# A depthwise convolution of width 31 moved from vector instructions to 32x32 matmul tiles, inside a one-layer hybrid backbone

## The chip, the core and the metric

The kernel runs on one core of a Trainium2 chip. The core has five engines that take their instructions in order and wait for each other through semaphores: TensorE (PE in the profile; its weight loads are listed as PEld), VectorE (DVE), ScalarE (ACT), GpSimd (POOL) and SyncE (SP, which here only issues DMAs). The metric is the time of one execution on the device in microseconds; the smaller, the better. Matmul results land in PSUM, which this kernel cuts into eight banks of 128x512 fp32; everything else lives in SBUF or in HBM.

## What is computed

The layer has 512 latent tokens of width 1024 and 256 context tokens. One projection `w_in` feeds a state-space branch (S5), a convolution branch and two gates; the branches are merged, and a mixture of 32 experts follows. The change touches the convolution branch alone:

```python
def conv_branch(zb, n_rows, w_dw, b_dw, ln_g, ln_b, w_out):
    v = glu(zb)
    n_b, n_l, ch = v.shape
    v = v.reshape(n_b * n_rows, n_l // n_rows, ch)
    v = lax.conv_general_dilated(v, w_dw.astype(v.dtype)[:, None, :], window_strides=(1,), padding='SAME',
                                 dimension_numbers=('NWC', 'WIO', 'NWC'), feature_group_count=ch) + b_dw
    v = jax.nn.silu(layernorm(v, ln_g, ln_b))
    return v.reshape(n_b, n_l, ch) @ w_out
```

Here `ch` is 512, there are 8 rows of 64 tokens, and the filter has 31 taps. Every channel has its own filter, so a channel of the output is a sum of 31 shifted copies of the same channel of the input, each times one number.

## The kernel before

Activations lie with channels on the 128 partitions and the 512 tokens along the row, so the 512 channels of the convolution are four blocks `j` = 0 to 3 of 128x512.

The stretch that matters comes after the projection of the S5 input and before the merge. Its loop is written as a list of one-letter steps, `RaAaODPBbUVTCkaI`, run for `b` = 0 to 7. On PE and ACT the instructions stand in the order in which these steps are written (a manual schedule); on DVE, POOL and SP a scheduler orders them when the program is built, by priority and readiness, and the engines then run that fixed order. The steps that the prediction speaks of:

- A, B and C are tiles of the `w_in` projection, `z_tile(t)` (lines 754 to 774): 24 matmuls of 128x128 by 128x512 into one PSUM bank (`zp`), from weights split into a high part `zuwh` (ACT, line 751) and a low part `zuwl` (DVE, for eight of the tiles POOL, line 752) two tiles ahead. Tiles 0 to 7 are the convolution's GLU: an even one is kept, an odd one is passed through a sigmoid and multiplied with the even one before it into the padded buffer `vp` (line 770). Tiles 8 to 23 are gates. Tiles 0, 1 and 2 run ahead of the loop.
- I is `s5_in(b+2)` (lines 658 to 694): 16 matmuls (`pv`, line 666), then some sixteen DVE instructions with two scans (line 681) among them and a few on POOL, which give `st`. R is `s5_read(b)` (line 699 on, `py`), which uses what I made two rounds earlier. k is `s5_pk(b+2)` (line 546), b the transposes of `s5_pv` (line 533), V and P prepare S5 tables on POOL and DVE, O transposes S5 results (line 720).
- a is one step of a product that is worked off on the side, `ada` (lines 806 to 846): either four 128x32 matmuls `pma` (line 818) that DVE adds up in `adacc`, or scalings on ACT and additions on POOL.

The convolution of block j is written as closures: `conv_taps(j)` (lines 783 to 789) appends one `tensor_scalar` (tap 0 and the bias) and 30 `scalar_tensor_tensor` to the list `taps`, each of which multiplies a shifted 128x512 view of `vp` with a column of taps and adds to `cacc`. `tap(200)` after the loop writes them all out at the end of the block, and the scheduler then places all 124 among the other DVE instructions, where it sees room. After the loop `cacc` goes through a layernorm (line 995 on: `pmu`, `pvr`) while the S5 branch runs through its GLU (`pglu`).

SBUF tiles of 128x512 come from one pool tag, `s2`, with seven buffers; PSUM has four banks of tag `mm` (`zp`, `py`), two of `s5` and two of `tp` (transposes, `pk`, `pma`, `padr`).

Of the kernel before, what the change touches and what calls it, by code (L numbers as in the profile page):

```python
# [9 lines left out]
F32 = mybir.dt.float32  # L10
# [3 lines left out]
AF = mybir.ActivationFunctionType  # L14
ALU = mybir.AluOpType
# [11 lines left out]
def hybrid_kernel(  # L27
# [9 lines left out]
    V, S, G, T, SY = nc.vector, nc.scalar, nc.gpsimd, nc.tensor, nc.sync  # L37
    D = 1024
    L, LC = 512, 256
# [7 lines left out]
    TAPS, HALF = 31, 15  # L47
    ROWS, RW = 8, 64
# [12 lines left out]
    hstack = ExitStack()  # L61
    hp = hstack.enter_context(tc.tile_pool(name="hp", bufs=1))
    smstack = ExitStack()
    sm = smstack.enter_context(tc.tile_pool(name="sm", bufs=7, side="right"))
    ps = ctx.enter_context(tc.tile_pool(name="ps", bufs=4, space=PSUM))

    def t2k(name, dt=F32, cols=512, p=128):
        return sm.tile([p, cols], dt, tag="s2", name=name)

    def t4k(name):  # L70
        return sm.tile([128, 1024], F32, tag="ub", name=name, bufs=2)

    def ps_mm(name, p=128):
        return ps.tile([p, 512], F32, tag="mm", name=name, bufs=4)
# [4 lines left out]
    def ps_tp(name, p=128):  # L79
        return ps.tile([p, 512], F32, tag="tp", name=name, bufs=2)  # L80
# [114 lines left out]
    sel32 = sm.tile([128, 32], F32, tag="sel32", name="sel32", bufs=1)  # L195
# [4 lines left out]
    cwt = const.tile([128, 4, 32], F32, name="cwt")  # L200
# [7 lines left out]
    def col(nm, j):  # L208
        return cols[:, ROW[nm] + j:ROW[nm] + j + 1]
# [185 lines left out]
    def mm3(acc, wh, wl, ah, al, start, stop):  # L395
        T.matmul(acc, lhsT=wh, rhs=ah, start=start, stop=False)  # L396
        T.matmul(acc, lhsT=wh, rhs=al, start=False, stop=False)  # L397
        T.matmul(acc, lhsT=wl, rhs=ah, start=False, stop=stop)  # L398
# [318 lines left out]
    def s5_out(j):  # L717
        pt = ps_tp("pt")
        for t in range(TC):
            T.transpose(pt[:, 64 * t:64 * t + 64], ysb[j][:, t, :], ident[0:64, 0:64])  # L720
        y = sm.tile([128, L], F32, tag="yt", name="yt", bufs=1)
        S.activation(y.rearrange("p (c t) -> p c t", t=TC), pt.rearrange("p (t c) -> p c t", t=TC), AF.Copy)
        S.activation(yh[:, j, :], y, AF.Copy)
        V.tensor_tensor(yl[:, j, :], y, yh.bitcast(F32)[:, j, :], op=ALU.subtract)
# [17 lines left out]
    def z_load(t):  # L742
        if t < len(zt) and zt[t][0] not in zraw:
            zraw[zt[t][0]] = wload(f"zr{t}", w_in[0], zt[t][0])

    def z_split(t):
        if t < len(zt):
            c0, i, _ = zt[t]
            raw = zraw[c0][:, :, 128 * i:128 * i + 128]
            zu[t] = wpair(0, list(raw.shape[1:]), "zu")  # L750
            S.activation(zu[t][0], raw, AF.Copy)
            (G if t in ZPOOL else V).tensor_tensor(zu[t][1], raw, zu[t][0].bitcast(F32), op=ALU.subtract)  # L752

    def z_tile(t):
        z_split(t + 2)
        z_load(t + 4)
        w = zu.pop(t)
        c0, i, kind = zt[t]
        acc = ps_mm("zp")
        for k in range(KD):  # L760
            mm3(acc, w[0][:, k, :], w[1][:, k, :], hh[:, k, :], hl[:, k, :], k == 0, k == KD - 1)
        if kind == "a":
            zp.append(acc)
            return

        sg = t2k("sg")
        S.activation(sg, acc, AF.Sigmoid)  # L767
        if kind == "b":
            jb = t // 4
            V.scalar_tensor_tensor(vp[jb][:, i, :, HALF:HALF + RW], sg.rearrange("p (r t) -> p r t", r=ROWS), 0.0,  # L770
                                   zp.pop().rearrange("p (r t) -> p r t", r=ROWS), op0=ALU.add, op1=ALU.mult)
            conv_taps(2 * jb + i)
        else:
            SY.dma_start(out=gd[2 * kind + i], in_=sg)

    gd = dram.tile([16, 128, L], F32, name="gd")
    cacc = {}
    taps = []

    for j in range(2):  # L780
        cacc[j] = t4k("cacc").rearrange("p (a n) -> p a n", a=2)

    def conv_taps(j):
        src = vp[j // 2][:, j % 2]
        dst = cacc[j // 2][:, j % 2, :].rearrange("p (r t) -> p r t", r=ROWS)
        e = V
        taps.append(lambda: e.tensor_scalar(dst, src[:, :, 0:RW], cwt[:, j, 0:1], col("conv_b", j), op0=ALU.mult, op1=ALU.add))
        for k in range(1, TAPS):
            taps.append(lambda k=k: e.scalar_tensor_tensor(dst, src[:, :, k:k + RW], cwt[:, j, k:k + 1], dst, op0=ALU.mult, op1=ALU.add))  # L789

    def tap(n):
        for _ in range(min(n, len(taps))):
            taps.pop(0)()

    adr = dram.tile([8, 512], F32, name="adr")

# [75 lines left out]
    with tc.manual_schedule(engines=MANM):  # L872
        def zt_(t):
            if t < 24:
                z_tile(t)

        def in_(b):
            if b < NB:
                inp[b] = s5_in(b)

        def if_(f, b):
            if b < NB:
                f(b)

        MID = {"R": lambda b: s5_read(b, *inp.pop(b)), "U": lambda b: s5_ut(b + 2), "P": lambda b: if_(s5_pa, b + 2), "a": lambda b: ada(1),
               "A": lambda b: zt_(3 * b + 3), "B": lambda b: zt_(3 * b + 4), "C": lambda b: zt_(3 * b + 5),
               "O": lambda b: s5_out(b // 2) if b % 2 else None, "D": lambda b: if_(s5_bd, b + 2), "b": lambda b: if_(s5_pv, b + 2),
               "k": lambda b: if_(s5_pk, b + 2), "V": lambda b: if_(s5_vb, b + 3), "T": lambda b: if_(s5_pt, b + 2), "I": lambda b: in_(b + 2)}
        M0 = {"s0": lambda: z_split(0), "s1": lambda: z_split(1), "z0": lambda: z_tile(0), "z1": lambda: z_tile(1), "z2": lambda: z_tile(2),
              "i0": lambda: in_(0), "i1": lambda: in_(1), "bd1": lambda: s5_bd(1), "pt1": lambda: s5_pt(1), "pv1": lambda: s5_pv(1),  # L890
              "pk1": lambda: s5_pk(1), "vb2": lambda: s5_vb(2), "pv0": lambda: s5_pv(0), "pk0": lambda: s5_pk(0), "pt0": lambda: s5_pt(0),
              "vb1": lambda: s5_vb(1), "pa1": lambda: s5_pa(1), "bd0": lambda: s5_bd(0)}
        for o in (
                "s0 z0 pt1 s1 bd1 z1 i0 pv1 i1 vb2 pk1 z2"
        ).split():
            if o not in done:
                M0[o]()
                done.add(o)
        assert not set(M0) - done, set(M0) - done
        for b in range(NB):  # L900
            for o in 'RaAaODPBbUVTCkaI':
                MID[o](b)
        tap(200)
    s5stack.close()
    hstack.close()
    e1 = ctx.enter_context(tc.tile_pool(name="e1", bufs=3, reuse_waits="tile"))
# [331 lines left out]
    n = 0  # L1238
# [153 lines left out]
    with tc.If(n_gen > 0):  # L1392
        with tc.For_i(0, n_gen, 1):
# [16 lines left out]
            n = 0  # L1410
# [35 lines left out]
            for q in range(4):  # L1446
                t = w_part(q)
# [8 lines left out]
            for k in range(2):  # L1456
                t = w_part(4 + k)
# [110 lines left out]
    with tc.manual_schedule(engines=MAN):  # L1568
# [12 lines left out]
        for e in range(NE + 1):  # L1581
# [32 lines left out]
            if 0 < e < NE - 1:  # L1614
                y = tile_y(pd)
# [64 lines left out]
```

## Time and profile before

| | |
|---|---|
| device time, median of 3 runs | 921.58 us (921.26 to 922.81) |
| the profiled execution | 921.29 us; span from its first to its last instruction 919.6 us |
| PE busy over the span | 752.9 us (82%) |
| DVE busy | 781.4 us (85%) |
| ACT busy | 532.7 us (58%) |
| POOL busy | 385.7 us (42%) |
| mean granted TensorE clock | 0.916 of full speed |

The program falls into four stretches: start and first projection up to about 116 us, the loop with the convolution to about 397 us, the branches' output, merge and routing to about 560 us, and the experts to the end. Shares over the whole span say little, since the stretches have different limits; in the loop one reads which engine has no idle time, and what the others wait for.

### The profile page before, as it was taken

Reading aid. Unit: us, or ns where it says so; the run is one execution under the profiler, and the core shown is the slowest. Engines: PE = TensorE matmul, PEld = TensorE weight load, DVE = VectorE, ACT = ScalarE, POOL = GpSimd, SP = SyncE. Lnnn points to the kernel's source line nnn. Section 1 sums busy time; section 2 is a strip of 40 time slices with the busy share of each in tenths; the row PEclk is TensorE's granted clock in tenths of the full one; section 3 lists DMA queues with packets and bytes.
Section 4 is the critical chain, followed back from the end, with each engine's and each line's share of the span. In section 5 each row is a group of like instructions: output and inputs, shape, how many; then the busy total and the mean of one; then the engine's idle time right before and its main releaser. Section 6 shows DMA issues by size and latency. Waiting matters only on the chain. (4 is left out here: it accounts for less than half of the span.)

```text
span 919.6 us, 12129 instructions
## 1 busy us (share of the span) xinstructions
PE 752.9 (82%) x4070; PEld 592.3 (64%) x4070; DVE 781.4 (85%) x1030; ACT 532.7 (58%) x819; POOL 385.7 (42%) x291
## 2 busy tenths in 40 slices
PE   3598986693569668489899985999999999999972
PEld 0476774482447556356688864788888888888751
DVE  4848489999999999997874596999999999999867
ACT  4444533353525528228532343988888888888752
POOL 4555448376745766412600222123333233333443
PEclk9998997897779879789999996999999999999986
DMA  8925952322353333378777346989999998988232
GB/s 310 244 92 156 240 183 86 118 84 74 92 166 111 105 129 113 111 243 312 241 263 274 138 161 204 384 338 372 327 381 359 376 396 319 352 311 324 67 128 92
DMA packets 89981, 201.75 MB, mean 219 GB/s; under 512 B 12558, under 2 KB 42320, under 8 KB 85810
## 3 DMA queue, kind: packets, MB, share of 16 engines
q1 hardware_dynamic: 82658, 180.00, 55.9%
q0 software_dynamic: 4832, 12.44, 3.8%
q10 hardware_dynamic: 2416, 8.44, 3.5%
q8 instruction: 32, 0.52, 0.2%
q14 instruction: 43, 0.35, 0.1%
HBM read 180.16 MB, written 22.76 MB: 221 GB/s over the span
## 5 line engine op out<-in xcount | busy, mean ns | idle before, releaser
L1276 DVE TENSOR_TENSOR ewwl<-eraw,ewwh 128x1024 fp32r<-128x1024 f32 x96 | 120.2, 1253 | 8.0 <-ACT ewwh L1271 5.2
L1271 ACT ACTIVATE ewwh<-eraw 128x1024 fp32r<-128x1024 f32 x96 | 101.9, 1063 | 6.6 <-issue 4.3
L398 PE MATMUL zp<-hh,zuwl 128*128 128x512 f32 x192 | 82.1, 428 | 21.1 <-POOL zuwl L752 21.0
L1299 POOL DMA_INDIRECT xg<-h2d,tb x32 | 48.3, 1510 | 112.3 <-PE ped L1346 87.2
L396 PE MATMUL zp<-hh,zuwh 128*128 128x512 f32 x192 | 84.6, 441 | 0.0
L1303 POOL DMA_INDIRECT ybuf<-ye,tb x30 | 42.5, 1417 | 94.3 <-ACT ye L1354 93.2
L397 PE MATMUL zp<-hl,zuwh 128*128 128x512 f32 x192 | 81.7, 426 | 0.0
L1290 DVE TENSOR_TENSOR edl<-eraw,edh 128x1024 fp32r<-128x1024 f32 x64 | 75.4, 1218 | 5.5 <-ACT edh L1286 5.5
L1323 PE MATMUL peg<-ewwh,st 128*128 128x512 f32 x192 | 77.5, 404 | 0.0
L1324 PE MATMUL peg<-ewwh,st 128*128 128x512 f32 x192 | 77.0, 401 | 0.0
L1325 PE MATMUL peg<-ewwl,st 128*128 128x512 f32 x192 | 76.9, 400 | 0.0
L1286 ACT ACTIVATE edh<-eraw 128x1024 fp32r<-128x1024 f32 x64 | 67.8, 1061 | 10.2 <-PE ped L1349 10.1
L789 DVE SCALAR_TENSOR_TENSOR cacc<-vpch,cwt,cacc 128x512 f32<-128x512 f32 x60 | 66.2, 1131 | 0.1
L789 DVE SCALAR_TENSOR_TENSOR cacc<-vpcl,cwt,cacc 128x512 f32<-128x512 f32 x60 | 61.0, 1042 | 0.5
L398 PEld LDWEIGHTS zp<-hh,zuwl 128*128 128x128 f32 x192 | 40.4, 210 | 32.5 <-POOL zuwl L752 22.8
L98 POOL TENSOR_TENSOR adacc<-adacc,wa 128x512 f32<-128x512 f32 x30 | 49.2, 1641 | 20.9 <-ACT wa L827 19.6
L767 ACT ACT_TABLE_LOAD x14 | 18.0, 1283 | 69.0 <-DVE b L688 25.6
L1346 PE MATMUL ped<-edh,at 128*128 128x512 f32 x128 | 53.2, 416 | 1.4 <-ACT at L1338 1.4
L1347 PE MATMUL ped<-edl,at 128*128 128x512 f32 x128 | 50.2, 392 | 0.0
L396 PEld LDWEIGHTS zp<-hh,zuwh 128*128 128x128 f32 x192 | 41.0, 214 | 13.4 <-issue 4.7
L397 PEld LDWEIGHTS zp<-hl,zuwh 128*128 128x128 f32 x192 | 40.6, 212 | 8.5
L1325 PEld LDWEIGHTS peg<-ewwl,st 128*128 128x128 f32 x192 | 36.7, 191 | 9.1
(486 smaller groups left out, 2189.7 us busy)
## 6 DMA issues: line engine op xcount, KB each, us to landing
eraw<-in_w_exp_down_dram SPq DMA_DIRECT2D x31, 1024.0 KB, 8.7
eraw<-in_w_exp_gate_dram SPq DMA_DIRECT2D x61, 512.0 KB, 7.2
eraw<-in_w_exp_up_dram SPq DMA_DIRECT2D x61, 512.0 KB, 7.9
wa<-in_w_ada_dram SPq DMA_DIRECT2D x32, 512.0 KB, 3.8
zr<-in_w_in_dram SPq DMA_DIRECT2D x12, 1024.0 KB, 5.7
wa<-in_w_ada_dram SPq DMA_DIRECT2D x8, 1024.0 KB, 11.3
ybuf<-zero ACTq DMA_DIRECT2D x4, 1024.0 KB, 7.1
gd<-sg SPq DMA_DIRECT2D x16, 256.0 KB, 5.8
```

The costliest lines, as they stand in the source:

```text
L396: T.matmul(acc, lhsT=wh, rhs=ah, start=start, stop=False)
L397: T.matmul(acc, lhsT=wh, rhs=al, start=False, stop=False)
L398: T.matmul(acc, lhsT=wl, rhs=ah, start=False, stop=stop)
L789: taps.append(lambda k=k: e.scalar_tensor_tensor(dst, src[:, :, k:k + RW], cwt[:, j, k:k + 1], dst, op0=ALU.mult, op1=ALU.add))
L1271: S.activation(hi, src, AF.Copy)
L1276: i = V.tensor_tensor(lo, src, hi.bitcast(F32), op=ALU.subtract)
L1286: S.activation(u[0], r[2][:, q, :], AF.Copy)
L1290: i = V.tensor_tensor(u[1], r[2][:, q, :], u[0].bitcast(F32), op=ALU.subtract)
L1323: T.matmul(pg, lhsT=st[:, k, 0, :], rhs=w_h[:, k2, :], start=(k == 0), stop=False)
L1324: T.matmul(pg, lhsT=st[:, k, 1, :], rhs=w_h[:, k2, :], start=False, stop=False)
L1325: T.matmul(pg, lhsT=st[:, k, 0, :], rhs=w_l[:, k2, :], start=False, stop=(k == KD - 1))
L1346: T.matmul(pd[h], lhsT=at[:, k, 0, :], rhs=w_h[:, hs[h]], start=(k == 0), stop=False)
```

## The change

Each tap becomes a matmul with a diagonal matrix. `conv_diag(j)` builds, for block j, the taps as diagonals of 32x32 matrices (two DVE instructions: the identity pattern `sel32` times the taps). `conv_taps(j)` then issues 31 x 4 = 124 matmuls of 32 rows by 32 columns over 512 tokens: the 32-channel group r goes through row group r of the array, tap k through column group k modulo 4, so that 16 places of the array are named in turn. Group r collects in its own PSUM bank, each column group in its own quarter of the partitions: 8 taps (7 in one quarter) add up in each quarter. Four ACT copies bring the banks to SBUF, and `conv_sum(j)` adds the four quarters by one matmul per group with `sel32` (four matmuls of 128x32) and adds the bias in an ACT instruction that writes `cacc`.

`conv_part(t)`, called at the end of each `z_tile`, issues `conv_taps` after tiles 2, 4, 6, 8 and `conv_sum` after tiles 3, 5, 7, 9. The list `taps` and the call `tap(200)` go. The `s2` tag gets an eighth buffer, and the S5 result tile `yt` moves into that tag. Nothing else in the program is written differently.

```diff
-    sm = smstack.enter_context(tc.tile_pool(name="sm", bufs=7, side="right"))
+    sm = smstack.enter_context(tc.tile_pool(name="sm", bufs=8, side="right"))
...
-        y = sm.tile([128, L], F32, tag="yt", name="yt", bufs=1)
+        y = t2k("yt")
...
         if kind == "a":
             zp.append(acc)
+            conv_part(t)
             return
...
-            conv_taps(2 * jb + i)
         else:
             SY.dma_start(out=gd[2 * kind + i], in_=sg)
+        conv_part(t)
...
+    def conv_diag(j):
+        cdg[j] = []
+        for k0 in (0, 16):
+            n = min(16, TAPS - k0)
+            t = t2k("cdg").rearrange("p (k c) -> p k c", c=32)
+            V.tensor_tensor(t[:, 0:n], sel32.unsqueeze(1).to_broadcast([128, n, 32]), cwt[:, j, k0:k0 + n].unsqueeze(2).to_broadcast([128, n, 32]), op=ALU.mult)
+            cdg[j].append(t)
+
     def conv_taps(j):
         src = vp[j // 2][:, j % 2]
-        dst = cacc[j // 2][:, j % 2, :].rearrange("p (r t) -> p r t", r=ROWS)
-        e = V
-        taps.append(lambda: e.tensor_scalar(dst, src[:, :, 0:RW], cwt[:, j, 0:1], col("conv_b", j), op0=ALU.mult, op1=ALU.add))
-        for k in range(1, TAPS):
-            taps.append(lambda k=k: e.scalar_tensor_tensor(dst, src[:, :, k:k + RW], cwt[:, j, k:k + 1], dst, op0=ALU.mult, op1=ALU.add))
...
+        conv_diag(j)
+        d = cdg.pop(j)
+        banks = [ps_mm("cp0"), ps_mm("cp1"), ps_tp("cp2"), ps_tp("cp3")]
+        for k in range(TAPS):
+            c = 32 * (k % 4)
+            for r in range(4):
+                rs_ = slice(32 * r, 32 * r + 32)
+                T.matmul(banks[r][c:c + 32], lhsT=d[k // 16][rs_, k % 16, :], rhs=src[rs_, :, k:k + RW], start=(k < 4), stop=(k >= TAPS - 4), skip_group_check=True)
+        cpart[j] = []
+        for r in range(4):
+            t = t2k("cpt")
+            S.activation(t, banks[r], AF.Copy)
+            cpart[j].append(t)
+
+    def conv_sum(j):
+        pc = ps_tp("pcv")
+        for r, t in enumerate(cpart.pop(j)):
+            T.matmul(pc[32 * r:32 * r + 32], lhsT=sel32, rhs=t, start=True, stop=True, skip_group_check=True)
+        S.activation(cacc[j // 2][:, j % 2, :], pc, AF.Identity, bias=col("conv_b", j))
+
+    def conv_part(t):
+
+        if 2 <= t < 10:
+            (conv_sum if t % 2 else conv_taps)((t - 2) // 2)
...
-        tap(200)
```

PE, at the end of tile 2, in the changed program: the last taps of block 0 (`cp` are its banks, `cdg` the diagonals) now stand ahead of `s5_read(0)` (line 704), which directly followed the last matmul of tile 2 (line 398) before.

```order
486 L804 MATMUL cp_1255<-vpch,cdg 32x512
487 L704 MATMUL py<-cl_707,st_1102 64x128 x2
488 L704 MATMUL py<-cl_708,st_1103 64x128 [waits Pool_49]
489 L704 MATMUL py<-cl_708,st_1103 64x128
490 L707 MATMUL py<-m,ut 64x128 [waits DMAHW7_49]
```

The first of these 124 matmuls (row 363 of PE's list) waits for DVE and POOL, so `s5_read(0)` and all that follows it on PE now stand behind that wait.

DVE, the same place, as a difference: ahead of the piece stand the two `s5_in` steps that run before the loop and the first instruction of `s5_vb` (`vta`).

```order
 L95 TENSOR_TENSOR vta<-bb,lv 128x512
+L553 TENSOR_TENSOR ks<-pk,ks 128x16
+L792 TENSOR_TENSOR cdg<-sel_157,cwt 128x512
+L792 TENSOR_TENSOR cdg<-sel_157,cwt 128x480
+L847 COPY adacc<-pma 128x256
+L752 TENSOR_TENSOR zuwl<-zr_1037,zuwh 128x1024
+L492 TENSOR_SCALAR tb_1466<-sin 128x512
```

The diagonals of block 0 stand where the third tap of block 0 stood, behind all of `s5_in(0)` and `s5_in(1)`; behind them DVE's next instruction waits for `pma`, which PE issues after the taps.

DVE once more, the end of `s5_in(2)` (`st`) in the changed program.

```order
L95 TENSOR_TENSOR st_1795<-b_1797,b_1798 64x256
L95 TENSOR_TENSOR st_1795<-b_1797,b_1798 64x4x64
L752 TENSOR_TENSOR zuwl<-zr_1487,zuwh 128x1024
L792 TENSOR_TENSOR cdg<-sel_157,cwt 128x512
L792 TENSOR_TENSOR cdg<-sel_157,cwt 128x480
```

The diagonals of block 2 stand behind the whole of `s5_in(2)` and one split of weights; the taps of block 2 follow tile 6 on PE.

## Rows read from the trace of the kernel before

**Rows 1.** The page: DVE's busy share in tenths, 40 slices of 23 us.
```profile
DVE  4848489999999999997874596999999999999867
```
**Rows 2.** Busy time by stretch: us, then PE, PEld, DVE, ACT, POOL, clock, DMA.
```profile
129.00:200.00 71.00, 52.93 (x377) 40.75 (x378) 70.86 (x76) 33.37 (x59) 44.96 (x30) 0.86 0.28 88
200.00:396.20 196.20, 129.58 (x838) 100.18 (x834) 194.87 (x209) 86.01 (x150) 122.08 (x83) 0.82 0.38 118
396.20:425.60 29.40, 25.49 (x127) 15.21 (x124) 24.11 (x32) 14.28 (x22) 6.74 (x9) 0.94 0.77 268
```
**Rows 3.** PE's waits from 118 to 425 us: who waited for whom, us, times, longest.
```profile
PE zp L398 <- POOL zuwl L752: 21.0, 3, 12.3
PE pv L533 <- DVE adb L841: 13.6, 1, 13.6
PE pma L818 <- DVE ks L553: 9.5, 1, 9.5
PE pma L818 <- DVE adacc L822: 8.0, 1, 8.0
PE pt L720 <- DVE ks L553: 7.3, 1, 7.3
PE pt L720 <- DVE adacc L822: 6.0, 1, 6.0
...
PE padr L840 <- DVE adacc L820: 3.4, 1, 3.4
```
**Rows 4.** Groups of instructions: busy us, mean ns, idle before.
```profile
L789 DVE SCALAR_TENSOR_TENSOR cacc<-vpch,cwt,cacc 128x512 f32<-128x512 f32 x60 | 66.2, 1131 | 0.1
L789 DVE SCALAR_TENSOR_TENSOR cacc<-vpcl,cwt,cacc 128x512 f32<-128x512 f32 x60 | 61.0, 1042 | 0.5
...
L95 DVE TENSOR_TENSOR vta<-bb,lv 128x512 f32<-128x512 f32 x8 | 9.7, 1215 | 0.0
...
L535 ACT ACTIVATE vt<-pv 128x512 f32<-128x512 f32 x16 | 8.8, 596 | 22.7 <-PE pv L533 22.7
```
**Rows 5.** PE's timeline around its first loop round: start us, us, instructions.
```profile
119.31 1.13 PE L533 MATMUL pv<-ident,vb 128*128 128x128 f32 x8
120.81 1.97 PE L666 MATMUL pv<-ut,vt 128*64 128x128 f32 x32 [0.37 <-ACT vt L535]
122.71 0.72 PE L546 MATMUL pk<-cl,bd 64*32 64x144 f32 x32
123.36 0.50 PE L396 MATMUL zp<-hh,zuwh 128*128 128x512 f32 x1
...
129.03 0.66 PE L704 MATMUL py<-cl,st 128*64 128x128 f32 x8
...
130.49 0.64 PE L818 MATMUL pma<-wa,condz 128*32 128x256 f32 x8
131.06 0.50 PE L396 MATMUL zp<-hh,zuwh 128*128 128x512 f32 x1
```
**Rows 6.** PE's timeline, `s5_read(2)` and `s5_read(7)`.
```profile
200.02 0.61 PE L704 MATMUL py<-cl,st 128*64 128x128 f32 x8
...
396.17 0.66 PE L704 MATMUL py<-cl,st 128*64 128x128 f32 x8
```
**Rows 7.** PE's timeline after an idle stretch: matmuls of tile 4.
```profile
145.84 0.63 PE L398 MATMUL zp<-hh,zuwl 128*128 128x512 f32 x1
146.26 0.61 PE L396 MATMUL zp<-hh,zuwh 128*128 128x512 f32 x1
```
**Rows 8.** PE's timeline: fp32 products of the layernorm, three matmuls as six passes.
```profile
421.06 2.73 PE L1006 MATMUL pvr<-sq,ones 128*128 128x512 f32 x6
```
**Rows 9.** DVE's timeline: end of `s5_in(1)`; first and last steps of `s5_in(2)`.
```profile
142.39 0.15 DVE L553 TENSOR_TENSOR ks<-pk,ks 128x16 f32<-128x16 f32 x1
...
177.38 0.68 DVE L669 TENSOR_TENSOR a<-pv,cos 128x512 f32<-128x512 f32 x1
...
185.93 1.65 DVE L752 TENSOR_TENSOR zuwl<-zr,zuwh 128x1024 fp32r<-128x1024 f32 x1
```

More of the change, by code (lines that the diff above doesn't have):

```diff
@@ L771, in z_tile @@
                                    zp.pop().rearrange("p (r t) -> p r t", r=ROWS), op0=ALU.add, op1=ALU.mult)
-            conv_taps(2 * jb + i)
         else:
             SY.dma_start(out=gd[2 * kind + i], in_=sg)
+        conv_part(t)
     gd = dram.tile([16, 128, L], F32, name="gd")
     cacc = {}
-    taps = []
     for j in range(2):
         cacc[j] = t4k("cacc").rearrange("p (a n) -> p a n", a=2)
+    cdg, cpart = {}, {}
+    def conv_diag(j):
[5 more added lines that the diff above has]
+            cdg[j].append(t)
     def conv_taps(j):
         src = vp[j // 2][:, j % 2]
-        dst = cacc[j // 2][:, j % 2, :].rearrange("p (r t) -> p r t", r=ROWS)
-        e = V
-        taps.append(lambda: e.tensor_scalar(dst, src[:, :, 0:RW], cwt[:, j, 0:1], col("conv_b", j), op0=ALU.mult, op1=ALU.add))
-        for k in range(1, TAPS):
-            taps.append(lambda k=k: e.scalar_tensor_tensor(dst, src[:, :, k:k + RW], cwt[:, j, k:k + 1], dst, op0=ALU.mult, op1=ALU.add))
-    def tap(n):
-        for _ in range(min(n, len(taps))):
-            taps.pop(0)()
+        conv_diag(j)
[19 more added lines that the diff above has]
+            (conv_sum if t % 2 else conv_taps)((t - 2) // 2)
     adr = dram.tile([8, 512], F32, name="adr")
```

## The prediction

> **What bounds the kernel now.** I read the profile from the whole to the place. The page first: DVE's tenths are at 9 in every slice from the sixth to the eighteenth, about 115 to 410 us, and nowhere else in a run as long until the experts [rows 1]. That is the loop with the convolution. The busy times by stretch say the same more sharply: DVE works 70.86 of 71 us and 194.87 of 196.2 us, while PE idles 18 of the 71 and 66.6 of the 196.2, and POOL is busy 122 [rows 2]. So DVE sets the pace there; the question is what stands next behind it.
>
> The waits of PE answer part of that: six rows name DVE (13.6, 9.5, 8.0, 7.3, 6.0 and 3.4, together 47.8 us), the longest names POOL's weight splits (21.0 us) [rows 3]. Each DVE row is a small instruction (`ks`, `adacc`, `adb`) that PE needs to free a PSUM bank, and that sat in a full DVE queue.
>
> **What is removed.** 120 taps of 1131 and 1042 ns, 66.2 + 61.0 = 127.2 us [rows 4], and four first taps priced alike, 4 us: 131 us of DVE, of the 290 that it works in the three stretches [rows 2]. Added are 8 products for the diagonals; their nearest row is `vta`, also a product of two broadcast operands of that size, 1.2 us [rows 4]: 10 us. DVE is left with some 169 us of work in 297 us and stops being the bound.
>
> **What is added on PE.** The main price, and no row shows a 32x32 tile. The nearest is `pk`, fp32 tiles of 64 rows by 32 columns, eight places in turn. An fp32 matmul runs as two passes (three matmuls are six passes), and a pass over 512 columns costs at most 2.73/6 = 0.455 us [rows 8]. A pass over `pk`'s 144 columns is then 0.128 us, and its 32 passes would take 4.1 us one by one; from the start of `pk` to the next matmul pass 0.65 us [rows 5]. That is four rounds of eight (0.51 us) and 0.14 us to fill and empty: all eight places work at once, with four different streams on the same rows. 124 taps are 248 passes; 16 at a time that is 15.5 rounds of 0.455 = 7.05, with the ends 7.2 us per block at full clock. The ends of the range: eight at a time, the most that a row shows, 14.2 us; four at a time (row groups one after another, as `pma`'s 8 passes of 256 columns in 0.57 us [rows 5] show for columns alone) 28.4 us. None can be below 7.05, since 16 places is all there are. I take 7.2, since `pk`'s eight show no loss from either direction of the split. At the lower clock each would double: matmuls 0.42 us apart after an idle stretch [rows 7] against 5.67/24 = 0.236 in a warm tile [rows 5].
>
> The Trainium skill ("TensorE: Matmul & The Clock Gate", Part 3, the table of measured speedups) gives 16 tiles of 32x32 a speedup of 10.6, not 16. By it a block would take 248 x 0.455 / 10.6 = 10.6 us, an estimate from that page, and the sum below would be 14 us longer; the trace, with eight of eight at work, speaks for the smaller price.
>
> `conv_sum`: 8 passes, four at a time like `pma`: 2 x 0.455 + 0.15 = 1.1 us. The ACT copies: 128x512 from PSUM take 596 ns [rows 4], four 2.4 us, and with 4 for `cacc` 20 copies, 12 us on an engine that is busy 86 of 196 us [rows 2]: no bound. But the copies hold both `tp` banks, so `pma`, `pk` or the transposes that follow on PE wait for them: 2.4 us per block. The eighth buffer and `yt` in its tag cost and give nothing that a row shows; four buffers of the eight are held from the copies to the sum, which tightens `s5_in`, but its result is wanted a round later, so a round of PE work covers it.
>
> **What moves: walk along PE.** One loop round on PE at full clock, from rows 5: three tiles of 5.67 us (123.36 to 129.03), 17.0; the others by their starts in the same way, `py` 1.46; `pma` 0.57 twice; transposes 1.13, and half of that for every second round's; `pk` 0.65; `pv` 1.90. Sum 23.9 us. Before, a round took (396.17 - 200.02)/5 = 39.2 us [rows 6].
>
> 1. Tile 2 ends at 129.03. The taps of block 0 need their diagonals, which stand on DVE behind `s5_in(0)`, `s5_in(1)` and `ks`. Before, DVE was through with those at 142.5 [rows 9]; less two taps ahead of them (2.2), plus one diagonal (1.2): 141.5. PE waits 12.5 us, where it waited 5.7 before, and all behind it on PE waits too. Taps 7.2, and 2 for the clock that has fallen: 150.7.
> 2. To `py(1)`: `py` 1.46 (its bank is a free `mm`), 1.0 more until the copies are done, `pma` 0.57, tile 5.67, sum 1.1, `pma` 0.57, tile 5.67, taps 7.2, copies 2.4, transposes 1.13, tile 5.67, sum 1.1, `pk` 0.65, `pma` 0.57, `pv` 1.9 = 36.7: 187.4.
> 3. `py`, `pma`, tile: 195.1. The diagonals of block 2 stand behind `s5_in(2)`, 177.38 to 187.58 in the rows before [rows 9], 10.2 us, plus 1.2: ready at 198.8, a wait of 3.7. Taps 7.2 and 1 for the clock: 207.0. Then copies, `pma`, two sets of transposes, two tiles, a sum, taps, copies, `pk`, `pv`, 29.8: `py(2)` at 236.8. Before it was at 200.0. **So far the change has lost 37 us.**
> 4. Five rounds without taps: 23.9 each, 1.1 for the last sum, and the last round without transposes, `pk` and `pv`, 4.3 less: 116.3 us if PE never waits. Before they took 196.2, with 66.6 idle. How much idle remains is my choice: between none and half (33 us, and 6 for clock lost after waits). POOL has 122 us of work there, a good part for `ada` and S5 tables that the change leaves alone, so waits do not vanish. I take a quarter, 17 us, and 3 for the clock: 136. `py(7)` at 373 instead of 396.2: 23 us gained.
> 5. From there to 425.6 PE works 25.5 of 29.4 us [rows 2], and the S5 GLU and the layernorm's products stay. What goes is the wait of 3.4 for `adacc` [rows 3] and some 2.6 of slow clock behind it: 6 us. The merge and the experts behind run on PE and shift as a whole: nothing.
>
> Sum: 23 + 6 = 29 us. The profiled execution took 921.3 us, 1.7 more than its span and 0.3 under the median; the difference goes along unchanged. **892 us.** With no waits left in step 4 it is 872, with half of them 911.
>
> **The rivals.**
>
> *Eight places at a time.* `pk` shows eight and cannot show more. Then 7.0 us more per block: 892 + 28 = 920, no change within what can be told.
>
> *Row groups one after another; slower.* Four tiles that share columns but lie in different rows would take turns, because each group's 32 rows stream their own data and `pk` proves only two groups side by side. 28.4 us per block, 21.2 more, four times: 85 us, 977. The point from which the sign turns: the gain of 29 us is used up at 7.2 more per block, that is when fewer than eight places work at once. Against it: both row halves of `pk` ran fully together.
>
> *One matmul after another, in order.* The second pass of each tap would wait for its first in the same place, nothing behind it could start meanwhile, and only neighbours would overlap: 125 steps of 0.455 = 57 us per block, 199 us more in all, 1091. The trace speaks against it: `pk`'s 16 matmuls would have needed 17 steps of 0.128, 2.2 us, where 0.65 passed [rows 5]. The Trainium skill ("PSUM — Partial Sum Buffer", Engine vs sequencer instructions) has such a rule: matmuls start and complete in program order. Taken so, with the two passes of a matmul one behind the other, the trace does not agree.
>
> *DVE was not what held PE; POOL and ACT are.* DVE's queue empties, but PE goes on waiting for POOL's splits and for S5 tables: the 21.0 us already name POOL [rows 3], and 122 us of POOL in a stretch of 136 would be 90%. With half of the waits left and another 4 us: 915. For the other side: of POOL's own idle time most must be time behind DVE, since nearly all it reads comes from there.
>
> **How the numbers follow.** The walk with none to half of the waits left, 872 to 911: 0.62, and 892 in it. POOL and ACT hold PE: 0.12, 905 to 925. Eight at a time, 905 to 935: 0.13. Row groups in turn: 0.10, near 977. In order: 0.03, near 1091. The range reaches from 4 us below the walk's lower end to past the middle of eight at a time: 868 to 925 leaves out some 0.02 below and, above, the upper part of the third case (0.04) and the two last (0.13). A measurement of this kernel can tell about 0.2% (1.8 us) from no change. Faster: all of the first case, four fifths of the second, half of the third: 0.62 + 0.10 + 0.06 = 0.78. Within 0.2%: 0.04, from the second and third. Slower: the rest, 0.18.
>
> **What would show it.** In the trace of the changed kernel: line 804 in four bursts of about 7 us (14, 28 or 57 name the rivals); PE idle for about 12 us ahead of the first burst with a diagonal as releaser, and 3 to 4 ahead of the third; `py(2)` near 237 and `py(7)` near 373; DVE at some 80% in the loop instead of 99%; and PE's waits naming POOL and ACT more than DVE. Wrong would be: bursts over 14 us, `py(2)` past 250, rounds over 30 us behind the taps, or a change in the experts' stretch, where I expect none.

## The result, and the profile after

The changed kernel takes 909.92 us in the median (908.42 to 911.29), the kernel before beside it 921.42 (920.53 to 922.81): a ratio of 0.987, with a 95% interval from 0.985 to 0.989. So it is faster, by 11.5 us where the prediction said 29. The profiled execution has a span of 907.8 us, where before had 919.6.

The page of the changed kernel: busy times, then DVE's tenths and the granted clock's.

```profile
PE 778.0 (86%) x5094; PEld 602.4 (66%) x5094; DVE 677.7 (75%) x914; ACT 543.7 (60%) x839; POOL 375.9 (41%) x291
...
DVE  4948473473599778637874596999999999999867
...
PEclk9988987999989998989999987999999999999976
```

The unbroken row of nines that stood in [rows 1] is gone; DVE works 3 to 9 tenths in those slices. The stretches of [rows 2], with the third one moved by 11 us to where it now lies (us, then PE, PEld, DVE, ACT, POOL, clock, DMA):

```profile
129.00:200.00 71.00, 52.83 (x761) 35.86 (x760) 40.98 (x51) 25.11 (x47) 34.60 (x25) 0.90 0.25 79
200.00:385.00 185.00, 156.41 (x1492) 117.41 (x1494) 133.88 (x139) 105.81 (x182) 123.28 (x94) 0.94 0.42 130
385.00:414.00 29.00, 22.97 (x100) 12.32 (x97) 10.69 (x12) 13.74 (x21) 4.86 (x4) 0.88 0.76 268
```

PE is now busy 156.4 of 185 us where it was busy 129.6 of 196.2, and DVE 133.9 (72%) where it had 1.3 us of idle time in all. POOL has the same work as before (123 us) in less time. PE's waits from 118 to 425 us, which answer to [rows 3]:

```profile
PE cp L804 <- DVE cdg L792: 17.8, 3, 12.6
PE pv L533 <- DVE adb L868: 5.3, 1, 5.3
PE pk L546 <- DVE cl L95: 5.1, 1, 5.1
PE pma L845 <- DMA wa<-in_w_ada_dram: 4.5, 1, 4.5
PE pt L720 <- ACT ys L712: 4.0, 1, 4.0
PE pma L845 <- ACT ks L551: 3.5, 3, 1.8
...
PE zp L398 <- POOL zuwl L752: 0.2, 1, 0.2
```

The 13.6 for `adb` has become 5.3, the waits for `ks` and `adacc` on DVE are nearly gone, and so is the longest row of before, 21.0 us for POOL's splits (now 0.2). First now is a wait that the change itself brought: 17.8 us for the diagonals `cdg`, 12.6 of it ahead of the first block. The four tap bursts on PE's timeline (start us, us, instructions, idle before and its releaser), one line from each place:

```profile
141.60 10.41 PE L804 MATMUL cp<-vpch,cdg 32*32 32x512 f32 x248 [12.58 <-DVE cdg L792]
...
167.04 8.71 PE L804 MATMUL cp<-vpch,cdg 32*32 32x512 f32 x248
...
200.74 11.34 PE L804 MATMUL cp<-vpcl,cdg 32*32 32x512 f32 x248 [3.38 <-DVE cdg L792]
...
231.30 8.71 PE L804 MATMUL cp<-vpcl,cdg 32*32 32x512 f32 x248 [1.84 <-DVE cdg L792]
```

The starts of `s5_read(b)`, the `py` products of [rows 6], are the milestones along PE by which the kernels below are compared. They are read from PE's timeline of each kernel; the last column is its span less py(7), which is everything behind the loop. The kernels under the second are the experiments.

```
kernel                  py(0)  py(1)  py(2)  py(3)  py(7)  py(3) to py(7)  py(7) to end
before                  129.0  167.2  200.0  244.8  396.2      151.4          523.4
changed                 151.9  189.6  244.6  277.2  383.9      106.7          523.9
before_one_tap          129.9  160.6  186.5  224.4  339.4      115.0          524.4
after_four_taps         143.2  175.8  217.7  249.6  356.4      106.8          524.8
taps_two_tiles_later    129.4  176.9  231.8  281.3  388.1      106.8          524.7
after_eight_places      157.8  200.8  266.4  298.7  405.2      106.5          524.5
after_half_columns      156.7  201.1  269.8  301.3  408.3      107.0          521.9
no_side_weights         152.5  190.2  245.7  272.1  385.8      113.7          519.9
diagonals_early         150.8  188.2  236.9  270.5  377.1      106.6          523.5
early_and_bank          138.8  179.6  229.1  262.7  369.4      106.7          524.1
bank_alone              154.4  192.2  247.7  281.3  387.9      106.6          523.7
```

Two readings of this table carry most of what follows. Behind the taps, four rounds take 106.5 to 107 us in the changed kernel and in seven of the eight experiments made on it, whatever the first rounds do. And the part behind py(7) lasts about as long in the kernel before as in nearly all others: the 6 us that the prediction had gained there do not exist.

### The profile page after: what moved, and what is told of

Same layout as the page of the kernel before. It is cut to its first block, busy times and chain, and to the rows that moved or that the text cites. A ratio compares the mean times of both kernels' runs of the same rounds, so it can differ in the third digit from the quotient of the medians.

```text
span 907.8 us, 14079 instructions
## 1 busy us (share of the span) xinstructions
PE 778.0 (86%) x5094; PEld 602.4 (66%) x5094; DVE 677.7 (75%) x914; ACT 543.7 (60%) x839; POOL 375.9 (41%) x291
## 4 chain that ended last, share of the span: by engine, by line
PE 53%; DVE 14%; issue 9%; DMA 9%; POOL 8%; ACT 4%; SPq 3%; ACTq 0%; POOLq 0%; DVEq 0%
PE peg L1351 6%; PE peg L1349 6%; PE peg L1350 6%; DMA wa<-in_w_ada_dram 4%; PE cp L804 3%; PE ped L1372 3%; PE pxt L1337 3%; PE ped L1373 3%; PE ped L1375 3%; POOL adacc L98 2%; PE po L1192 2%; PE po L1191 2%; PE po L1190 2%; DVE so L681 1%; DVE st L95 1%
## 5 line engine op out<-in xcount | busy, mean ns | idle before, releaser
L396 PE MATMUL zp<-hh,zuwh 128*128 128x512 f32 x192 | 78.1, 407 | 0.0
L398 PE MATMUL zp<-hh,zuwl 128*128 128x512 f32 x192 | 76.3, 398 | 0.4 <-POOL zuwl L752 0.2
L397 PE MATMUL zp<-hl,zuwh 128*128 128x512 f32 x192 | 75.9, 395 | 0.0
L98 POOL TENSOR_TENSOR adacc<-adacc,wa 128x512 f32<-128x512 f32 x30 | 46.2, 1540 | 41.4 <-ACT wa L854 39.0
L808 ACT ACTIVATE cpt<-cp 128x512 f32<-128x512 f32 x16 | 8.3, 602 | 61.3 <-PE cp L804 49.7
L396 PEld LDWEIGHTS zp<-hh,zuwh 128*128 128x128 f32 x192 | 36.9, 192 | 11.6 <-issue 4.4
L398 PEld LDWEIGHTS zp<-hh,zuwl 128*128 128x128 f32 x192 | 36.6, 191 | 9.5 <-POOL zuwl L752 1.6
L1350 PEld LDWEIGHTS peg<-ewwh,st 128*128 128x128 f32 x192 | 36.4, 190 | 8.9 <-DVE st L1340 0.4
L1349 PEld LDWEIGHTS peg<-ewwh,st 128*128 128x128 f32 x192 | 36.5, 190 | 8.6 <-ACT st L1339 0.3
L397 PEld LDWEIGHTS zp<-hl,zuwh 128*128 128x128 f32 x192 | 36.8, 192 | 7.2
```

The source lines that it names most:

```text
L1349: T.matmul(pg, lhsT=st[:, k, 0, :], rhs=w_h[:, k2, :], start=(k == 0), stop=False)
L1350: T.matmul(pg, lhsT=st[:, k, 1, :], rhs=w_h[:, k2, :], start=False, stop=False)
```

## Experiments

**What relieving DVE is worth by itself.** In the kernel before, the closures of taps 1 to 30 are left out.

```diff
-        for k in range(1, TAPS):
+        for k in range(1, 1):
             taps.append(lambda k=k: e.scalar_tensor_tensor(dst, src[:, :, k:k + RW], cwt[:, j, k:k + 1], dst, op0=ALU.mult, op1=ALU.add))
```

> The kernel before with 30 of the 31 taps of each block left out (only the first tap is computed), so VectorE is relieved as in the changed kernel and TensorE gets nothing in exchange. Theory A, VectorE's stream sets the loop before: from py(0) to py(7) (129.0 to 396.2) VectorE loses about 105 us of its 265 busy, TensorE's 182 busy become the bound, and of TensorE's 85 idle us there half or more go: time falls by 42 to 60 us, to 862 to 880. Rival B, another chain (the weights of the side product, the weights' rounding on ScalarE) stands right behind VectorE: the time falls by under 25 us, to 897 or more. What the time falls by is the gross gain of the change, out of which its TensorE work is paid.

Measured: 864.08 us, ratio 0.937 (0.934 to 0.941). Theory A. The gross gain is 58 us; the changed kernel keeps 11.5 of it, so its own work and waits cost 46.

**What the taps cost on PE.** In the changed kernel only taps 0 to 3 are computed.

```diff
-        for k in range(TAPS):
+        for k in range(4):
             c = 32 * (k % 4)
...
-                T.matmul(banks[r][c:c + 32], lhsT=d[k // 16][rs_, k % 16, :], rhs=src[rs_, :, k:k + RW], start=(k < 4), stop=(k >= TAPS - 4), skip_group_check=True)
+                T.matmul(banks[r][c:c + 32], lhsT=d[k // 16][rs_, k % 16, :], rhs=src[rs_, :, k:k + RW], start=(k < 4), stop=True, skip_group_check=True)
```

> The changed kernel with 27 of the 31 taps of each block left out (taps 0 to 3 only, one for each column group); diagonals, copies and sums are kept. The four tap bursts took 10.4, 8.7, 11.4 and 8.7 us; with 1/8 of the passes they should take about 1.2 each, 34 us less in all. Theory A, every us of a burst counts in full: the time falls by 28 to 36 us, to 874 to 882. Rival B, the waits of TensorE later in the loop and the side product's weights take it back: it falls by under 17 us, to 893 or more. The 12.6 us wait for the diagonals ahead of the first burst stays in both.

Measured: 881.76 us, ratio 0.955 (0.952 to 0.958), 28 us below the changed kernel's median. The four bursts took 2.13, 1.16, 2.02 and 1.17 us, 6.5 in all where they had been 39.2. Theory A: what a burst takes counts almost in full, 32.7 us less on PE and 28 less in the time. A burst at full clock, on PE's timeline of this kernel:

```profile
158.99 1.16 PE L804 MATMUL cp<-vpch,cdg 32*32 32x512 f32 x32
```

216 passes more take 8.71 - 1.16 = 7.55 us more, 35 ns each on average. They do not come evenly. How many of a burst's passes have begun by a moment is read from two stretches of the second burst of the changed kernel (`cp` instructions on PE: stretch, its length, PE busy and passes, clock, DMA):

```profile
167.04:168.81 1.77, 1.77 (x64) 1.00 0.00 0
167.04:174.09 7.05, 7.05 (x224) 1.00 0.46 152
```

The first 64 passes, four in each of the 16 places, begin within 1.77 us: 0.44 us a pass in each place, so that up to there 16 places lose nothing against the eight of the next experiment. The following 160 take 5.28 us, one in 33 ns on average. The 32 passes of the short burst lie wholly in the stretch without loss, so this experiment prices the burst and says nothing on the slower pace.

**Whether 16 places stream at once.** The tap goes to column group k modulo 2, so that 8 places are used; copies and sum take 64 partitions (the flags and the sum's product follow).

```diff
-            c = 32 * (k % 4)
+            c = 32 * (k % 2)
...
-            S.activation(t, banks[r], AF.Copy)
+            S.activation(t[0:64], banks[r][0:64], AF.Copy)
```

> The changed kernel with two column groups and not four (8 of the 16 places; the copies and the sum take 64 partitions). The computation is the same. Each place now has 31 passes of 0.428 us in a row, 13.3 us, and not 15.5 passes, 6.6 us; the bursts of the changed kernel took 8.7 at full clock. Theory A, a place streams without gaps and the 8.7 came from handing out passes one by one to 16 places: a burst takes 13.3 to 14.3 us here. Rival B, each place loses a quarter of its time whatever the number of places: 17 us or more. Time: four bursts together 20 us longer by A (about 926 to 932), 35 us longer by B (about 940 to 946).

Measured: 931.52 us, ratio 1.011 (1.008 to 1.013), bursts of 15.92, 13.94, 16.75 and 13.94 us. The second, on PE's timeline of this kernel:

```profile
172.98 13.94 PE L804 MATMUL cp<-vpch,cdg 32*32 32x512 f32 x248
```

Theory A. 31 passes in each place take 13.94 us, 0.450 us a pass: the price of a pass that the prediction used (0.455), with eight of eight places at work all the time. With 16 places the same price would give 15.5 x 0.450 = 7.0 us, and it was 8.71: behind the first 64 passes something else is the limit. With eight places the kernel would have been slower than before; the prediction's first rival had it at 920.

**Passes or columns.** Each tap product is cut into two of 256 columns, so that the places stream the same number of columns in twice as many passes. (The two halves share a bank and set its start flag separately; the sums that come out are not the convolution's, but every pass runs.)

```diff
-                T.matmul(banks[r][c:c + 32], lhsT=d[k // 16][rs_, k % 16, :], rhs=src[rs_, :, k:k + RW], start=(k < 4), stop=(k >= TAPS - 4), skip_group_check=True)
+                for h in range(2):
+                    T.matmul(banks[r][c:c + 32, 256 * h:256 * h + 256], lhsT=d[k // 16][rs_, k % 16, :], rhs=src[rs_, 4 * h:4 * h + 4, k:k + RW], start=(k < 4), stop=(k >= TAPS - 4), skip_group_check=True)
```

> The changed kernel with each tap product cut into two of 256 columns (496 passes in a burst and not 248, each half as long). The computation is the same. Theory A, with 16 places the passes are handed out at some 35 ns each (8.71 us / 248) and that sets a burst: 496 passes take 17 to 17.6 us at full clock, about twice. Rival B, what a burst takes is the columns that the places stream, plus a fixed start and end: it stays at 8.7 to 10 us. Time by A: some 33 us longer than the changed kernel (about 940 to 946), by B within 5.

Measured: 931.88 us in one run, 22 us longer than the changed kernel, between the two forecasts (33 by A, within 5 by B). The second burst, on PE's timeline of this kernel:

```profile
171.82 15.49 PE L805 MATMUL cp<-vpch,cdg 32*32 32x256 f32 x496
```

Nearer to A, though less than twice: 15.49/496 = 31 ns a pass, where 35 were expected. B is out: half as long passes at the old number of columns would have kept 8.7. So behind its start the number of passes sets a burst of 16 places: one in 33 ns with 512 columns, one in 31 with 256, although those are half as long. Why the pace falls to that after the first 64 was not found out. Each pass also loads its 32x32 weights, and the Trainium skill ("TensorE: Matmul & The Clock Gate", LDWEIGHTS) prices a weight load by its columns alone, which for 32 of them is an estimate of 27 ns from that page. Loads one after another would come near 31 to 33 ns, but the trace does not show them so: at the start of the second burst of the changed kernel 32 loads take 0.23 us, 7 ns each (PE's weight loads, timeline).

```profile
167.04 0.23 PEld L804 LDWEIGHTS cp<-vpch,cdg 32*32 32x32 f32 x32 [0.35 <-issue]
```

Whether loads hold the later passes stays open.

**The wait for the diagonals, first try.** Taps and sums are hung on the tile two later.

```diff
-        if 2 <= t < 10:
-            (conv_sum if t % 2 else conv_taps)((t - 2) // 2)
+        if 4 <= t < 12:
+            (conv_sum if t % 2 else conv_taps)((t - 4) // 2)
```

> The changed kernel with each block's taps and sums hung on the gate tile two later (taps at tiles 4, 6, 8, 10 and not 2, 4, 6, 8). The computation is the same. The first burst then stands behind py(0) and the diagonals have been built by then. Theory A, the waits for the diagonals (12.6, 3.4 and 1.8 us) count in full: these waits vanish, py(0) is back near 130, and the time falls by 12 to 18 us, to 892 to 898. Rival B, the time ahead of the first burst was no loss, since VectorE's chain sets when the second s5 round is ready anyway: the wait goes over into TensorE waits for other VectorE tiles and the time falls by under 5 us, to 905 or more.

Measured: 914.44 us, ratio 0.992 (0.989 to 0.995), not faster than the changed kernel. That decides nothing, because the waits did not vanish; they moved. From the list of those that waited for line 792, the diagonals (us, times):

```profile
  PE cp L804: 18.4, 4
```

`conv_taps` also places the diagonals, so they moved back on DVE's queue with the taps: 18.4 us in four waits in the place of 17.8 in three, the longest now ahead of the fourth burst (9.9). The run says nothing on A against B, only that where the diagonals stand in DVE's order is what counts. So the next kernel moves them alone.

**The diagonals alone.** Block 0's are built ahead of the first `s5_in`, in a sum tile that is still unused; the others one tile earlier.

```diff
-            t = t2k("cdg").rearrange("p (k c) -> p k c", c=32)
+            t = (t2k("cdg") if j else cacc[1][:, k0 // 16, :]).rearrange("p (k c) -> p k c", c=32)
...
-        conv_diag(j)
         d = cdg.pop(j)
...
         S.activation(cacc[j // 2][:, j % 2, :], pc, AF.Identity, bias=col("conv_b", j))
+        if j < 3:
+            conv_diag(j + 1)
...
-                "s0 z0 pt1 s1 bd1 z1 i0 pv1 i1 vb2 pk1 z2"
+                "s0 z0 pt1 s1 bd1 z1 cd i0 pv1 i1 vb2 pk1 z2"
```

> The changed kernel with its diagonals built earlier: block 0's in the storage of a sum tile that is not yet in use, ahead of the first s5 round in VectorE's queue (near 110 us, where VectorE sat idle for 6 us), those of blocks 1 to 3 one gate tile earlier. The computation is the same. Theory A, the waits for diagonals (12.6, 3.4, 1.8 us) and the low clock behind them (bursts of 10.4 and 11.3 where the others took 8.7) are the loss in the first rounds: bursts start without a wait, all take about 8.7, py(3) comes at 257 to 262 (277.2 in the changed kernel, 281.3 with the taps two tiles later), and the time falls to 890 to 896. Rival B, the first rounds are held by VectorE's chain behind the diagonals, whatever the taps do: py(3) stays past 270, TensorE waits for other VectorE tiles in the place of the diagonals, and the time stays at 904 or more. In both the stretch from py(3) to py(7) stays near 106.7 us and the one behind py(7) near 524.

Measured: 903.72 us, ratio 0.980 (0.978 to 0.982), at the edge of B's range and far from A's. The waits of 3.4 and 1.8 us are gone and with them the slow third burst (8.71 where it was 11.34). The first burst tells why it was no more. PE's timeline there:

```profile
128.67 1.74 PE L803 MATMUL cp<-vpch,cacc 32*32 32x512 f32 x6
140.18 10.66 PE L803 MATMUL cp<-vpch,cacc 32*32 32x512 f32 x242 [9.78 <-DVE ks L553]
```

What DVE did in that kernel up to the release, on its timeline:

```profile
136.94 1.61 DVE L95 TENSOR_TENSOR st<-b,b 64x256 f32<-64x256 f32 x2
138.58 1.47 DVE L95 TENSOR_TENSOR vta<-bb,lv 128x512 f32<-128x512 f32 x1
139.96 0.17 DVE L553 TENSOR_TENSOR ks<-pk,ks 128x16 f32<-128x16 f32 x1
```

It started at 128.7, as hoped, and stopped after six passes. Row groups 2 and 3 collect in `tp` banks, and one of these still held `pk`, whose last reader on DVE stands behind the second `s5_in`, at 140.0 to 140.1. In the changed kernel that read ended at 140.4 and the diagonals were built from 140.3 on, so that the profile showed only the later of the two. Neither theory had it.

**Both locks, and the bank alone.** `pk1` is moved ahead of `i1` on PE, so that DVE reads `pk` at the start of the second `s5_in` (at 129.97) and no longer behind it. Once this is done on top of the early diagonals, once in the changed kernel as it was.

```diff
-                "s0 z0 pt1 s1 bd1 z1 cd i0 pv1 i1 vb2 pk1 z2"
+                "s0 z0 pt1 s1 bd1 z1 cd i0 pv1 pk1 i1 vb2 z2"
```

> As the kernel with early diagonals, and on TensorE the kernel products pk of the second s5 block one place earlier, ahead of the block's input product: their bank (one that the first burst wants) is then read by VectorE ahead of the second s5 round and not behind it. The computation is the same. With early diagonals alone the first burst ran 6 passes at 128.7 and then sat until 140.2, when VectorE's last read of pk ended. Theory A, the bank was the second lock on the same door: the first burst starts near 129 and runs through in 8.7 to 9 us, py(0) at 137 to 140 (150.8), py(1) at 176 to 180 (188.2), and the time falls by 9 to 12 us against early diagonals alone, to 891 to 896. Rival B, the rounds behind are held by VectorE's second s5 round, so that the 10 us come back as other waits before py(2) (236.9): under 4 us, 900 or more.

> The changed kernel with only that move of pk (diagonals as late as in the changed kernel). The computation is the same. Theory A, two releases stand at about the same time (pk's read at 140.0 to 140.2, the first diagonals from 140.3 on), and either alone holds the burst: the wait of 12 us for the diagonals stays, and the time stays within 3 us of the changed kernel, 907 to 913. Rival B, the bank was the real lock and the profile names the diagonals only as the later of the two: the first burst starts before 136 and the time falls to 904 or less.

Measured: both locks away, 891.26 us, ratio 0.967 (0.965 to 0.970); the bank alone, 912.93, ratio 0.990 (0.987 to 0.993). Theory A in both. Ahead of the first burst the bank alone leaves 14.4 us of waiting for the diagonals, and the diagonals alone left 9.8 of waiting for the bank. With both away, the four bursts on PE's timeline:

```profile
130.15 8.71 PE L803 MATMUL cp<-vpch,cacc 32*32 32x512 f32 x248
...
157.00 8.71 PE L803 MATMUL cp<-vpch,cdg 32*32 32x512 f32 x248 [1.44 <-DVE vpch L771]
...
187.22 8.71 PE L803 MATMUL cp<-vpcl,cdg 32*32 32x512 f32 x248
...
214.28 8.71 PE L803 MATMUL cp<-vpcl,cdg 32*32 32x512 f32 x248
```

All four run at 8.71. Against the early diagonals alone the medians differ by 12.5 us, or 11.3 when each is set against the kernel before as measured beside it. The profiled execution was the slowest of this kernel's five (895.2; the others 887.8 to 895.0) and that of the early diagonals the fastest of its five (902.3). Between these two py(0) is 12.0 us earlier, py(1) 8.6 and py(7) 7.7: up to a third of the gain can be lost again in the second round, which is B's part. This kernel does the whole computation and is faster than both, the one before and the changed one.

**The tail.** In the changed kernel 30 of the 32 loads of `ada` weights are left out.

```diff
+            if m > 1:
+                araw[m] = awt[m % 2]
+                return
-            araw[m] = wp.tile([128, 2, 512], F32, tag="wx", name="wa3", bufs=2)
+            araw[m] = awt[m] = wp.tile([128, 2, 512], F32, tag="wx", name="wa3", bufs=2)
```

> The changed kernel with 30 of the 32 loads of the side product's weights left out (the two pieces loaded first are used again and again). Theory A, these loads hold the start of the tail (TensorE waited 4.5 us for one at 385.5, and pieces landed after 7.7 and 12.7 us): without them the stretch from py(7) to the end falls from 524 to 516 to 520, the loop by 0 to 3. Rival B, the tail's length is set by TensorE's own work and the experts' weights, and the side product only fills gaps: from py(7) to the end still 523 to 525, as in the five kernels so far (523.4 to 524.8).

Measured: 907.41 us in one run; py(7) to the end 519.9, at the upper end of A's range. By this run the loads hold some 4 us of the tail; `after_half_columns`, whose edit does not touch the tail, had 521.9, so that up to 2 us of it may be chance. The loop became 1.9 us longer (py(7) at 385.8, with 113.7 us from py(3) on), which was not followed up; so little of the 4 us reached the time.

## Why the prediction was right and wrong

The sign held, and so did the mechanism of the gain (DVE set the pace, PE pays for the taps); but of the 29 us forecast 11.5 came. In the profiles the miss is 7.8 us up to py(2), 3.3 from there to py(7), and 6.5 behind it. Two terms of the sum failed, and neither alone makes up the miss: the price of a burst (steps 2 and 3, 7.2 us where 8.71 was measured) and the 6 us that step 5 gained, of which nothing came.

*What bounds.* Right. DVE set the pace, and taking its taps away is worth 58 us gross (`before_one_tap`). Two rows were misread, without harm to the sum: the run of nines in [rows 1] begins with the seventh slice (138 us), not the sixth, and the full list behind [rows 3] has two more waits for DVE's `adacc`, 5.7 and 3.7 us, so that PE waited 57.2 us for such small instructions and not 47.8. DVE kept 185.6 us of work from 129 to 414, where the sum had 169; the diagonals took 14 of it, not 10.

*Step 1, the wait.* The walk gave 12.5 us for the diagonals; it was 12.6. Burst 10.4 at the low clock, against 9.2; py(0) 151.9 against 150.7 for the end of the taps. What the walk did not see is the second lock, the bank of `pk`. It cost nothing here, but whoever removes the first finds it.

*Steps 2 and 3, the price of a burst.* This is the term that was mis-sized first. 7.2 us at full clock was 8.71, and with the two cold ones four bursts took 39.2 us where the walk had 4 x 7.2 + 3 = 31.8: 7.4 us, of which 6.0 are the price at full clock and 1.3 the low clock. The waits ahead of the bursts came to 1.6 us more than in the walk, all the rest up to py(2) to 1.2 less. The chosen price assumed that 16 places work as `pk`'s eight do. Eight do (31 passes in a place take 13.94 us). Sixteen do for 64 passes and then no longer: from there on one pass came in 33 ns on average (31 in `after_half_columns`), and 16 places would need one in 28 (0.450/16). A `pk` of 32 passes could show neither the 16 places nor what comes behind the first 64. The Trainium skill's factor of 10.6 ("TensorE: Matmul & The Clock Gate", Part 3) came from the other side: 248 x 0.450 / 8.71 gives 12.8 here at full clock, and 11.4 over all four bursts (4 x 248 x 0.450 / 39.2). The measurement lies between the row that I extended and the figure that I set aside. The sum by that figure, 906, is nearer to the time, but with bursts dearer than they were and with the 6 us of step 5 still in it. I treated a row that shows eight as if it showed sixteen, though the text itself says that it cannot. The waits ahead of bursts 3 and 4 were 3.4 (3.7 expected) and 1.8 (none expected).

*Step 4.* 139.3 us for 136, with PE idle for 21.0 of them where the walk had 17: a good guess for what remained of PE's waits, for a partly wrong reason. The walk kept POOL's waits, and they went (21.0 to 0.2 us) with POOL's work unchanged; what is left are waits for DVE (`adb`, `cl`) and ACT. That POOL had been waiting for DVE is argued from this, not tested by itself.

*Step 5.* Wrong: nothing for 6 us. The 3.4 us wait for `adacc` went and a 4.5 us wait for weights of `ada` came in its place, and the slow clock behind a wait stayed. PE's timeline of the changed kernel behind py(7):

```profile
389.93 1.08 PE L845 MATMUL pma<-wa,condz 128*32 128x256 f32 x8 [4.46 <-DMA wa<-in_w_ada_dram]
390.76 1.91 PE L867 MATMUL padr<-adacc,ones 128*1 128x512 f32 x2
392.60 0.80 PE L396 MATMUL pglu<-yhl,glu0wh 128*128 128x512 f32 x1
393.19 0.63 PE L397 MATMUL pglu<-yhl,glu0wh 128*128 128x512 f32 x1
...
395.45 0.40 PE L398 MATMUL pglu<-yhl,glu0wl 128*128 128x512 f32 x1
```

I took a wait away without asking what is late next, as I had asked at the other stalls. `no_side_weights` shows some 4 us of it, in one run; the other 2.5 are not explained.

*Rivals.* Eight at a time, row groups in turn and strict order are out by the bursts. POOL holding PE is out by the 0.2 us; ACT does hold it, for 8.9 of the 21.0 us between py(2) and py(7), against 11.7 for DVE.

*What would show it.* Bursts of about 7: no, 8.7 to 11.3. Idle of 12 ahead of the first burst and 3 to 4 ahead of the third, with a diagonal as releaser: yes. py(2) near 237: 244.6, inside the 250 that was named. py(7) near 373: 383.9. DVE at 80% in the loop: 72% from 200 to 385 us, 65 from 129 to 414; the prediction's own sum, 169 us of 268, made 63. Rounds over 30 us behind the taps, named as a sign of being wrong: two of five (py(2) to py(3) 32.6, and 36.5 from 327.4 to 363.9), 27.9 on average, so that the even rounds of the walk were not there. Waits that name POOL and ACT more than DVE: no. No change in the experts: yes, they are part of the constant tail.

That `early_and_bank` lands at 891, beside the predicted 892, is no support for the sum: it gets there without the wait that the sum contains, and with bursts that are dearer than the sum's.

## What to carry to other kernels

Work moved from a full engine to the next one is paid there at full price: cost it there first, against the gross gain, and take the price of the new operation from a row that shows that many at once and for as long, or keep the range open to the next thing that limits it. Before an operation is moved to an early place, list everything that it needs there (operands, and the last reader of each bank that it takes over), since the profile names only the release that came last. A stall that is removed is a gain only if the next instruction in that queue has its data.

## What the runs showed of the hardware

Fp32 tiles of 32x32 ran eight at a time without loss (0.450 us a pass of 512 columns in each place). Sixteen at a time they did so for the first 64 passes (0.44 us); the passes behind came one in 33 ns with 512 columns and one in 31 with 256, and over a burst of 248 a fifth was lost.

The granted clock fell after a short wait. Busy time in the four bursts of the changed kernel (PE, PEld, DVE, ACT, POOL, clock, DMA):

```profile
141.60:152.00 10.40, 10.40 (x250) 6.12 (x252) 1.69 (x1) 0.00 (x0) 6.89 (x5) 0.82 0.11 31
167.00:175.70 8.70, 8.70 (x249) 5.32 (x248) 3.95 (x2) 0.00 (x0) 2.99 (x2) 1.00 0.37 123
200.70:212.10 11.40, 11.34 (x248) 6.38 (x248) 2.19 (x4) 0.02 (x1) 0.00 (x0) 0.74 0.01 3
231.30:240.00 8.70, 8.70 (x248) 5.33 (x248) 2.69 (x1) 0.01 (x1) 2.17 (x1) 1.00 0.10 34
```

Behind 3.4 us of idle the third burst got 0.74 of full speed, on average between the two levels of 1.2 and 2.4 GHz, and took 11.34 us; behind 1.8 us the fourth got 1.00. The first, behind 12.6 us, got 0.82, no worse than the third: a wait of 3.4 us cost 2.6 more in the burst behind it. That price varies: in `no_side_weights` and `bank_alone` the same wait of 3.38 us left a granted clock of 0.84 and 0.83, and the third burst took 10.24 and 10.27, 1.5 to 1.6 more.

The same kind of DVE instruction took very different times: the eight products for the diagonals 0.64 to 2.84 us, with a median of 1.76, where the prediction had 1.2 from `vta`. The line of the instructions that write `cdg` (durations in ns, least, median, most; first and last start):

```profile
L792 DVE TENSOR_TENSOR cdg<-sel,cwt x8: 644/1760/2835, 140.3 to 231.2; 128x512 f32<-128x512 f32 x4, 128x480 f32<-128x480 f32 x4
```

The traces show what goes with it. The changed kernel and `taps_two_tiles_later` have 16 of these products together. The four with no POOL instruction beside them took 0.64 to 0.68 us; each of the other twelve ended 0.51 to 0.55 us after the end of a POOL instruction that was under way when it began. One of the two longest, with the POOL instruction beside it (changed kernel), and a pair alone, behind the end of POOL's work at 254.33 (`taps_two_tiles_later`):

```profile
230.66 2.81 POOL L752 TENSOR_TENSOR zuwl<-zr,zuwh 128x1024 fp32r<-128x1024 f32 x1
231.17 2.81 DVE L792 TENSOR_TENSOR cdg<-sel,cwt 128x480 f32<-128x480 f32 x1
...
255.34 1.25 DVE L792 TENSOR_TENSOR cdg<-sel,cwt 128x512 f32<-128x512 f32 x2
```

By these traces what such a DVE instruction takes goes with the POOL instruction beside it; no run moved that POOL work away to test it.
